# Attention over short sequences on one core: another order of TensorE's work, transposes two chunks ahead, and Q left in key order until its scores are written

## The chip, the core and the metric

The kernel runs on one core of a Trainium2 chip. A core has several engines that run side by side and wait for each other through semaphores: TensorE (PE in the profile; PEld is its loading of weights), VectorE (DVE), ScalarE (ACT), GpSimd (POOL) and SyncE (SP). Transfers between the chip's memory (HBM) and the core's working memory (SBUF) are made by 16 DMA engines; here GpSimd issues the loads and SyncE the stores. TensorE writes its results into PSUM, eight banks of 2 KB in each of 128 partitions, from which DVE and ACT read.

The metric is the device time of one execution, in microseconds (us). For the kernel before it is 156.47 us, the median of three runs (156.12 to 156.62).

## The reference

```python
batch, n_heads, seq, head_dim = 32, 12, 128, 64      # q, k, v: float32
scale = 1.0 / np.sqrt(q.shape[-1])
scores = scale * np.matmul(q, k.transpose(0, 1, 3, 2))
scores_max = np.max(scores, axis=-1, keepdims=True)
attn = np.exp(scores - scores_max)
attn = attn / (np.sum(attn, axis=-1, keepdims=True) + 1e-8)
return np.matmul(attn, v).astype(np.float32)
```

There are 32 x 12 = 384 heads, each with 128 queries, 128 keys and 64 features. Three inputs of 12.58 MB are read and one output of that size is written. The kernel leaves out the subtraction of the row's maximum and the small constant; the inputs are small enough for exp without it. The row sums come out of the second matmul, through a column of ones behind the values.

## The kernel before

**Chunks.** The heads are handled 16 at a time, in 24 chunks (NCH = 24; A = 4 groups of partitions by CB = 4 heads each). A partition of a loaded Q or K tile holds runs of 16 consecutive rows of a head (4 KB of float32 in HBM), and a partition of a V or output tile runs of 4 rows (1 KB). These long runs mean that rows of a head are spread over partitions in an order of their own, and each step has to keep track of it.

**Loads.** All loads are issued at the start of the program by GpSimd (load_qk at L67, load_v at L75) and convert float32 to bf16 on the way. The input pool has as many buffers as there are chunks, so no load waits for compute. Their order is Q and K of chunk 0, V of chunk 0, then V, Q, K of chunks 1, 2 and so on; for the last chunk Q and K come before V, which is loaded in two halves.

**The work on a chunk c**, by function:
- turn(c, 0) and turn(c, 1), L102, DVE: two transposes each (one for each half of the 64 features, J = 2), which bring the features of Q and of K onto the partitions. Each writes 128 x 512 bf16 elements. The output pattern differs: ORDER[0] for Q puts the queries in output order, "tp g th", and so writes with a step of 4 elements in the innermost direction; ORDER[1] for K leaves "tp th g", whose innermost 8 elements are contiguous.
- scores(c), L114: 32 matmuls on TensorE, for 4 heads h, 2 feature halves j, and 4 row groups b of 32 partitions. Each writes 128 contiguous float32 of one row of s_ps. Behind them stands one exp on ACT (L119) over the whole s_ps, which gives attn in bf16. s_ps has a single buffer of four PSUM banks, so the next scores wait for this exp.
- values(c), L130 and L135: 16 matmuls with a permutation bring V's rows into the order of the keys, and ACT copies them into one of three v2 tiles, beside the column of ones.
- outputs(c, half), L147: 32 matmuls for two of the four heads. The columns of attn that they take as weights must be in output order, 32 contiguous ones for each t.
- finish(c, half, ...), L157 and L158, DVE: the reciprocal of the row sums and the multiplication into o_sb; then SyncE stores o_sb (L162), 512 KB for a chunk, or 256 KB for each half in the last two chunks.

The tiles of values and outputs share a pool of two PSUM buffers of two banks each (ps_w), in turn. The transposed tiles, attn and v2 have three buffers each, o_sb four.

**Order.** The program is scheduled by hand: each engine executes its instructions strictly in the order in which the main loop at L171 emits them. An iteration c emits scores(c), values(c+1), the Q transposes of c+1, both outputs of c, the first finish, the K transposes of c+1, the second finish. So on TensorE the outputs of c stand right behind the scores and the values that precede them, and on DVE the K transposes of c+1 stand between the two finishes of c.

Of the kernel before, what the change touches and what calls it, by code (L numbers as in the profile page):

```python
# [9 lines left out]
@with_exitstack  # L10
def kernel(
    ctx: ExitStack,
    tc: tile.TileContext,
    q: bass.AP,
    k: bass.AP,
    v: bass.AP,
    out: bass.AP,
):

    nc = tc.nc
    f32 = mybir.dt.float32
    bf16 = mybir.dt.bfloat16

    B, H, S, D = q.shape
    assert S == 128 and D == 64
    scale = 1.0 / (D ** 0.5)
    TQ = 16  # L30
    GQ = S // TQ
    T = 4
    A = 4
    G = S // T
    J = D // 32
    CB = 4
    NCH = B * H // (A * CB)

    def runs(x, t):
        return x.rearrange("b h (g t) d -> (b h g) (t d)", t=t).rearrange(  # L40
            "(n p) x -> p n x", p=128)

    qr, kr, vr, orr = runs(q, TQ), runs(k, TQ), runs(v, T), runs(out, T)

    singles = ctx.enter_context(tc.tile_pool(name="singles", bufs=1))
    pin = ctx.enter_context(tc.tile_pool(name="pin", bufs=NCH))
    pt = ctx.enter_context(tc.tile_pool(name="pt", bufs=3))
    pa = ctx.enter_context(tc.tile_pool(name="pa", bufs=3))
    po = ctx.enter_context(tc.tile_pool(name="po", bufs=4))
    ps_s = ctx.enter_context(tc.tile_pool(name="ps_s", bufs=1, space=bass.MemoryType.PSUM))  # L50
    ps_w = ctx.enter_context(tc.tile_pool(name="ps_w", bufs=2, space=bass.MemoryType.PSUM))

    NV2 = 3
    v2s = []
    for i in range(NV2):
        v2 = singles.tile([128, A, CB, D + 1], bf16, name=f"v2_{i}")
        nc.vector.memset(v2[:, :, :, D:D + 1], 1.0)  # L57
        v2s.append(v2)

    ORDER = ("p h (tp g th) -> p tp th h g", "p h (tp th g) -> p tp th h g")  # L60

    chunks, qts, attns, osbs = {}, {}, {}, {}

    def load_qk(c):
        for src, which in ((qr, 0), (kr, 1)):
            x = pin.tile([128, TQ, D], bf16, tag="qk"[which] + "_bf", name="qk"[which] + "_bf")
            nc.gpsimd.dma_start(out=x, in_=src[:, c, :].rearrange("p (t d) -> p t d", t=TQ))  # L67
            chunks[c, which] = x

    def load_v(c, parts=1):  # L70
        x = pin.tile([128, CB, T, D], bf16, tag="v_bf", name="v_bf")
        w = CB // parts
        for i in range(parts):
            n0 = c * CB + i * w
            nc.gpsimd.dma_start(  # L75
                out=x[:, i * w:(i + 1) * w],
                in_=vr[:, n0:n0 + w, :].rearrange("p n (t d) -> p n t d", t=T))
        chunks[c, 2] = x

    with tc.manual_schedule():  # L80
        load_qk(0)
        ident = singles.tile([128, 128], bf16)
        make_identity(nc, ident)
        perm = singles.tile([128, A, 4, GQ], bf16)
        nc.vector.tensor_copy(  # L85
            perm.rearrange("p a th g -> p a g th"),
            ident.rearrange("p (a g th) -> p a g th", a=A, th=4))

        load_v(0)
        for c in range(1, NCH):  # L90
            if c < NCH - 1:
                load_v(c)
            load_qk(c)
        load_v(NCH - 1, 2)

        def turn(c, which):


            x = chunks.pop((c, which))
            xt = pt.tile([128, J, 4, S], bf16, tag="qk"[which] + "t", name="qk"[which] + "t")  # L100
            for j in range(J):
                nc.vector.transpose(  # L102
                    xt[:, j].rearrange(ORDER[which], tp=4, th=4),
                    x[:, :, j * 32:(j + 1) * 32].rearrange("p (th tp) e -> p tp th e", tp=4))
            qts[c, which] = xt

        def scores(c):
            qt, kt = qts.pop((c, 0)), qts.pop((c, 1))
            s_ps = ps_s.tile([128, 4, 4, S], f32, tag="s_ps", name="s_ps")
            for h in range(4):  # L110
                for j in range(J):
                    for b in range(4):
                        pr = slice(b * 32, (b + 1) * 32)
                        nc.tensor.matmul(  # L114
                            s_ps[:, b, h, :], lhsT=kt[pr, j, h, :],
                            rhs=qt[pr, j, h, :], start=(j == 0), stop=(j == J - 1),
                            tile_position=(b * 32, 0))
            attn = pa.tile([128, 4, 4, S], bf16, tag="attn", name="attn")
            nc.scalar.activation(out=attn, in_=s_ps, func=mybir.ActivationFunctionType.Exp,  # L119
                                 bias=0.0, scale=scale)  # L120
            attns[c] = attn

        def values(c, n0=0, w=CB):

            v_bf = chunks[c, 2]
            v_ps = ps_w.tile([128, 1024], f32, tag="w_ps", name="v_ps")
            vp = v_ps[:, :A * w * D].rearrange("p (a n d) -> p a n d", a=A, n=w)
            for a in range(A):
                for t in range(T):
                    nc.tensor.matmul(  # L130
                        vp[t * G:(t + 1) * G, a],
                        lhsT=perm[:, a].rearrange("p th g -> p (th g)"),
                        rhs=v_bf[:, n0:n0 + w, t, :], start=True, stop=True,
                        tile_position=(0, t * G))
            nc.scalar.copy(v2s[c % NV2][:, :, n0:n0 + w, :D], vp)  # L135

        def outputs(c, half):
            attn = attns[c]
            v2 = v2s[c % NV2]
            o_ps = ps_w.tile([128, 1024], f32, tag="w_ps", name="o_ps")  # L140
            o2 = o_ps.rearrange("p (i x) -> p i x", i=2)
            ov = o2[:, :, :T * (D + 1)].rearrange("p i (t e) -> p i t e", t=T)
            for i in range(2):
                n = 2 * half + i
                for t in range(T):
                    for a in range(A):
                        nc.tensor.matmul(  # L147
                            ov[a * G:(a + 1) * G, i, t, :], lhsT=attn[:, n, a, t * G:(t + 1) * G],
                            rhs=v2[:, a, n, :], start=True, stop=True, tile_position=(0, a * G))
            return ov  # L150

        def finish(c, half, ov, store):
            if half == 0:
                osbs[c] = po.tile([128, CB, T, D], f32, tag="o_sb", name="o_sb")
            o_sb = osbs[c]
            recip = pa.tile([128, 2, T], f32, tag="recip", name="recip")
            nc.vector.reciprocal(recip, ov[:, :, :, D])  # L157
            nc.vector.tensor_mul(o_sb[:, 2 * half:2 * half + 2], ov[:, :, :, :D],  # L158
                                 recip.to_broadcast([128, 2, T, D]))
            if store:  # L160
                n0, n1 = 2 * (half + 1) - store, 2 * (half + 1)
                nc.sync.dma_start(  # L162
                    out=orr[:, c * CB + n0:c * CB + n1, :],
                    in_=o_sb[:, n0:n1].rearrange("p n t d -> p n (t d)"))

        e = NCH - 1
        turn(0, 0)
        turn(0, 1)
        scores(0)
        values(0)  # L170
        for c in range(e):  # L171
            if c > 0:
                scores(c)
            if c + 1 < e:
                values(c + 1)
            turn(c + 1, 0)
            o0 = outputs(c, 0)
            o1 = outputs(c, 1)
            finish(c, 0, o0, 2 if c == e - 1 else 0)
            turn(c + 1, 1)  # L180
            finish(c, 1, o1, 2 if c == e - 1 else CB)
        scores(e)
        values(e, 0, 2)
        values(e, 2, 2)
        o0 = outputs(e, 0)
        finish(e, 0, o0, 2)
        o1 = outputs(e, 1)
        finish(e, 1, o1, 2)
# [30 lines left out]
```

## Time and profile before

| | |
|---|---|
| time, median of three runs | 156.47 us (156.12 to 156.62) |
| the profiled execution, time | 156.66 us |
| the profiled execution, span | 154.9 us |
| busy: DVE / PE / ACT / POOL | 126.0 / 82.7 / 68.1 / 44.9 us |
| HBM read / written | 37.75 / 12.58 MB |
| mean granted TensorE clock | 0.549 of full speed |

The span runs from the first to the last instruction of the profile; the execution's own time is 1.76 us longer. The page divides the span into 40 slices and gives the busy share of each engine in tenths. The chain of work that ended last is followed back from the last instruction: at each step to what released it. In a row of the groups stand the line, the engine and operation, the tiles written and read with their shapes, the count, then the busy time with the mean duration of one in ns, then the idle time of the engine just before them and what ended most of it. In a row of the timeline or the chain stand the start and the duration in us first. A row of the windows gives the busy time (and count) of PE, PEld, DVE, ACT and POOL, the clock, the DMA engines' share and the GB/s.

### The profile page before, as it was taken

What the parts mean: (1) busy time and instruction counts of PE and PEld (TensorE: products, weight loads), DVE (VectorE), ACT (ScalarE), POOL (GpSimd) and SP (SyncE); (2) the same over time, 40 slices, a digit from 0 to 9 for tenths busy, and PEclk for the clock granted to TensorE, in tenths of its full rate; (3) what the DMA queues carried; (4) which work ended last, traced back from release to release, by engine and by line L of the source; (5) the groups of instructions that cost most, each with busy time, mean ns of one, the idle gap of its engine ahead of it and who ended that gap; (6) DMA issues with size and microseconds to landing.
All of it is one profiled execution on the core that took longest, in us unless ns stands there. A gap on an engine that the chain in (4) does not pass through costs nothing.

```text
span 154.9 us, 5909 instructions
## 1 busy us (share of the span) xinstructions
PE 82.7 (53%) x2704; PEld 53.5 (35%) x2704; DVE 126.0 (81%) x196; ACT 68.1 (44%) x50; POOL 44.9 (29%) x79
## 2 busy tenths in 40 slices
PE   0082565565565566556656556645746746644630
PEld 0051343343343343343343344333424424423420
DVE  1719988988988988988988988987988988988731
ACT  3054527527427427437337337337247256254150
POOL 7934434243333332331432332342231100000000
PEclk9999555555555555555555555555555555555555
DMA  3999999999999999999999999999999998134123
GB/s 47 172 189 204 206 223 231 247 228 237 243 229 232 247 229 231 245 230 228 247 229 228 247 229 231 244 229 232 248 225 236 237 248 227 38 134 138 69 72 135
DMA packets 32329, 31.84 MB, mean 206 GB/s; under 512 B 1584, under 2 KB 26160, under 8 KB 32304
## 3 DMA queue, kind: packets, MB, share of 16 engines
q0 software_dynamic: 19600, 18.88, 73.6%
q1 hardware_dynamic: 12704, 12.58, 28.2%
q8 instruction: 21, 0.34, 0.8%
q14 instruction: 4, 0.03, 0.1%
HBM read 37.75 MB, written 12.58 MB: 325 GB/s over the span
## 4 chain that ended last, share of the span: by engine, by line
DVE 34%; ACT 28%; PE 24%; DMA 5%; issue 4%; POOL 2%; ACTq 1%; POOLq 0%
ACT attn L119 28%; DVE kt L102 18%; PE s_ps L114 14%; DVE o_sb L158 11%; PE o_ps L147 10%; DMA q_bf<-in_q_dram 5%; DVE recip L157 3%; DVE qt L102 2%; POOL v_bf L75 1%; POOL k_bf L67 0%; ACTq L214 0%; POOL q_bf L67 0%; ACTq L119 0%; POOL ident masks.py:199 0%; POOL ident masks.py:197 0%
## 5 line engine op out<-in xcount | busy, mean ns | idle before, releaser
L119 ACT ACTIVATE attn<-s_ps 128x2048 bf16<-128x2048 f32 x24 | 45.0, 1877 | 80.5 <-PE s_ps L114 80.5
L102 DVE STREAM_TRANSPOSE qt<-q_bf 128x512 bf16<-128x512 bf16 x48 | 58.0, 1302 | 4.9 <-DMA q_bf<-in_q_dram 4.9
L114 PE MATMUL s_ps<-qt,kt 32*128 32x128 bf16 x768 | 29.4, 302 | 34.3 <-DVE kt L102 34.3
L147 PE MATMUL o_ps<-v,attn 128*32 128x65 bf16 x1536 | 29.9, 241 | 32.9 <-ACT attn L119 24.6
L147 PEld LDWEIGHTS <-attn 128*32 128x32 bf16 x1536 | 23.3, 125 | 46.7 <-ACT attn L119 36.5
L158 DVE TENSOR_TENSOR o_sb<-o_ps,recip 128x512 f32<-128x512 f32 x48 | 33.2, 691 | 1.7
L114 PEld LDWEIGHTS <-kt 32*128 32x128 bf16 x768 | 18.6, 129 | 42.3 <-DVE kt L102 42.3
L102 DVE STREAM_TRANSPOSE kt<-k_bf 128x512 bf16<-128x512 bf16 x48 | 31.1, 685 | 0.0
L130 PE MATMUL v_ps<-v_bf,perm 128*32 128x256 bf16 (+1 forms) x400 | 25.1, 406 | 0.3 <-DMA v_bf<-in_v_dram 0.3
L75 POOL DMA_DIRECT2D v_bf<-in_v_dram x25 | 18.8, 753 | 21.1 <-DMA q_bf<-in_q_dram 17.7
L135 ACT CAST v<-v_ps 128x1024 bf16<-128x1024 f32 (+1 forms) x25 | 24.2, 978 | 0.0
L67 POOL DMA_DIRECT2D k_bf<-in_k_dram x24 | 12.8, 534 | 38.3 <-DMA v_bf<-in_v_dram 37.4
L157 DVE RECIPROCAL recip<-o_ps 128x8 f32<-128x8 f32 x48 | 9.0, 188 | 16.0 <-PE o_ps L147 16.0
L67 POOL DMA_DIRECT2D q_bf<-in_q_dram x24 | 12.9, 539 | 16.0 <-DMA k_bf<-in_k_dram 13.8
L130 PEld LDWEIGHTS <-perm 128*32 128x32 bf16 x400 | 11.6, 130 | 7.4 <-issue 4.5
L85 DVE COPY perm<-ident 128x128 bf16<-128x128 bf16 x1 | 0.4, 446 | 2.0 <-POOL ident masks.py:199 2.0
L119 ACT ACT_TABLE_LOAD x1 | 1.3, 1283 | 0.7 <-PEq L203 0.7
L57 DVE MEMSET v<- 128x16 bf16 x3 | 0.2, 72 | 0.9 <-PEq L203 0.9
masks.py:199 POOL TENSOR_SCALAR_AFFINE_SELECT ident<-ident 128x128 bf16<-128x128 bf16 x1 | 0.3, 287 | 0.1
masks.py:197 POOL MEMSET ident<- 128x128 bf16 x1 | 0.2, 231 | 0.0
L203 POOL MEMSET const-float32-0.0<- 128x1 f32 x1 | 0.1, 93 | 0.2 <-issue 0.2
L203 POOL MEMSET const-bfloat16-1.0<- 128x1 bf16 x1 | 0.1, 95 | 0.0
(2 smaller groups left out, 0.2 us busy)
## 6 DMA issues: line engine op xcount, KB each, us to landing
out_dram<-o_sb SPq DMA_DIRECT2D x22, 512.0 KB, 9.1
q_bf<-in_q_dram POOLq DMA_DIRECT2D x24, 256.0 KB, 14.5
k_bf<-in_k_dram POOLq DMA_DIRECT2D x24, 256.0 KB, 13.5
v_bf<-in_v_dram POOLq DMA_DIRECT2D x23, 256.0 KB, 14.3
out_dram<-o_sb SPq DMA_DIRECT2D x4, 256.0 KB, 2.2
v_bf<-in_v_dram POOLq DMA_DIRECT2D x2, 128.0 KB, 13.5
```

The costliest lines, as they stand in the source:

```text
L57: nc.vector.memset(v2[:, :, :, D:D + 1], 1.0)
L67: nc.gpsimd.dma_start(out=x, in_=src[:, c, :].rearrange("p (t d) -> p t d", t=TQ))
L75: nc.gpsimd.dma_start(out=x[:, i * w:(i + 1) * w], in_=vr[:, n0:n0 + w, :].rearrange("p n (t d) -> p n t d", t=T))
L85: nc.vector.tensor_copy(perm.rearrange("p a th g -> p a g th"), ident.rearrange("p (a g th) -> p a g th", a=A, th=4))
L102: nc.vector.transpose(xt[:, j].rearrange(ORDER[which], tp=4, th=4), x[:, :, j * 32:(j + 1) * 32].rearrange("p (th tp) e -> p tp th e", tp=4))
L114: nc.tensor.matmul(s_ps[:, b, h, :], lhsT=kt[pr, j, h, :], rhs=qt[pr, j, h, :], start=(j == 0), stop=(j == J - 1), tile_position=(b * 32, 0))
L119: nc.scalar.activation(out=attn, in_=s_ps, func=mybir.ActivationFunctionType.Exp, bias=0.0, scale=scale)
L130: nc.tensor.matmul(vp[t * G:(t + 1) * G, a], lhsT=perm[:, a].rearrange("p th g -> p (th g)"), rhs=v_bf[:, n0:n0 + w, t, :], start=True, st ...
L135: nc.scalar.copy(v2s[c % NV2][:, :, n0:n0 + w, :D], vp)
L147: nc.tensor.matmul(ov[a * G:(a + 1) * G, i, t, :], lhsT=attn[:, n, a, t * G:(t + 1) * G], rhs=v2[:, a, n, :], start=True, stop=True, tile_ ...
L157: nc.vector.reciprocal(recip, ov[:, :, :, D])
L158: nc.vector.tensor_mul(o_sb[:, 2 * half:2 * half + 2], ov[:, :, :, :D], recip.to_broadcast([128, 2, T, D]))
```

## The change

Three things are changed.

1. The Q transposes take K's output pattern: the queries stay in the order "tp th g", as the keys do. ORDER is gone.
2. The score matmuls put them right: the right-hand operand is read in its own order, and the output in PSUM is addressed so that query (tp, th, g) lands at (tp, g, th). In the innermost direction, 8 elements g are then written with a step of 4 float32. exp, outputs and everything behind see s_ps as before.
3. The main loop is emitted in another order. Both turns of chunks 0 and 1 come first. An iteration c emits scores(c+1), both outputs of c, values(c+2), the Q transposes of c+2, the first finish of c, the K transposes of c+2, the second finish. The values of chunk 1 come in the first iteration, and those of the last chunk, in two halves, in the last one.

```diff
-    ORDER = ("p h (tp g th) -> p tp th h g", "p h (tp th g) -> p tp th h g")
...
                 nc.vector.transpose(
-                    xt[:, j].rearrange(ORDER[which], tp=4, th=4),
+                    xt[:, j].rearrange("p h (x g) -> p x h g", g=GQ),
                     x[:, :, j * 32:(j + 1) * 32].rearrange("p (th tp) e -> p tp th e", tp=4))
...
                         nc.tensor.matmul(
-                            s_ps[:, b, h, :], lhsT=kt[pr, j, h, :],
-                            rhs=qt[pr, j, h, :], start=(j == 0), stop=(j == J - 1),
+                            s_ps[:, b, h, :].rearrange("p (tp g th) -> p tp th g", tp=4, th=4),
+                            lhsT=kt[pr, j, h, :],
+                            rhs=qt[pr, j, h, :].rearrange("p (tp th g) -> p tp th g", tp=4, th=4),
+                            start=(j == 0), stop=(j == J - 1),
                             tile_position=(b * 32, 0))
...
         e = NCH - 1
-        turn(0, 0)
-        turn(0, 1)
+        for c in range(2):
+            turn(c, 0)
+            turn(c, 1)
         scores(0)
         values(0)
         for c in range(e):
-            if c > 0:
-                scores(c)
-            if c + 1 < e:
-                values(c + 1)
-            turn(c + 1, 0)
+            scores(c + 1)
+            if c == 0:
+                values(1)
             o0 = outputs(c, 0)
             o1 = outputs(c, 1)
+            if c + 2 < e:
+                values(c + 2)
+            elif c + 1 == e:
+                values(e, 0, 2)
+                values(e, 2, 2)
+            if c + 2 <= e:
+                turn(c + 2, 0)
             finish(c, 0, o0, 2 if c == e - 1 else 0)
-            turn(c + 1, 1)
+            if c + 2 <= e:
+                turn(c + 2, 1)
             finish(c, 1, o1, 2 if c == e - 1 else CB)
-        scores(e)
-        values(e, 0, 2)
-        values(e, 2, 2)
         o0 = outputs(e, 0)
         finish(e, 0, o0, 2)
         o1 = outputs(e, 1)
```

## The prediction

> **What bounds the kernel now.** I read the page's slices first, then the chain of waits, then GpSimd's timeline, which dates the landing of each load.
>
> ```profile
> span 154.9 us, 5909 instructions
> PE 82.7 (53%) x2704; PEld 53.5 (35%) x2704; DVE 126.0 (81%) x196; ACT 68.1 (44%) x50; POOL 44.9 (29%) x79
> ...
> DMA  3999999999999999999999999999999998134123
> GB/s 47 172 189 204 206 223 231 247 228 237 243 229 232 247 229 231 245 230 228 247 229 228 247 229 231 244 229 232 248 225 236 237 248 227 38 134 138 69 72 135
> ```
>
> Two things are nearly full: DVE, and the DMA engines up to slice 33. A slice is 154.9/40 = 3.87 us, so the loads are over at about 34 x 3.87 = 132 us. The last 23 us are compute that has fallen behind, with only stores left. One period of the chain, in order of time:
>
> ```profile
> 114.25 0.69 DVE o_sb L158
> 114.94 1.22 DVE kt L102 x2
> 116.17 0.05 issue
> 116.21 0.96 PE s_ps L114 x28
> 117.26 1.89 ACT attn L119
> 119.19 0.66 PE o_ps L147 x31
> 119.87 0.22 DVE recip L157
> 120.11 0.69 DVE o_sb L158
> ```
>
> It is a closed loop: K transposes, scores, exp, first half of the outputs, reciprocal, multiply, then the next K transposes. It takes 120.11 - 114.25 = 5.86 us and runs through three engines one after another. Within it DVE also does the Q transposes, while ACT and PE work. The groups give the work per chunk:
>
> ```profile
> L119 ACT ACTIVATE attn<-s_ps 128x2048 bf16<-128x2048 f32 x24 | 45.0, 1877 | 80.5 <-PE s_ps L114 80.5
> L102 DVE STREAM_TRANSPOSE qt<-q_bf 128x512 bf16<-128x512 bf16 x48 | 58.0, 1302 | 4.9 <-DMA q_bf<-in_q_dram 4.9
> L114 PE MATMUL s_ps<-qt,kt 32*128 32x128 bf16 x768 | 29.4, 302 | 34.3 <-DVE kt L102 34.3
> ...
> L158 DVE TENSOR_TENSOR o_sb<-o_ps,recip 128x512 f32<-128x512 f32 x48 | 33.2, 691 | 1.7
> ...
> L102 DVE STREAM_TRANSPOSE kt<-k_bf 128x512 bf16<-128x512 bf16 x48 | 31.1, 685 | 0.0
> ...
> L157 DVE RECIPROCAL recip<-o_ps 128x8 f32<-128x8 f32 x48 | 9.0, 188 | 16.0 <-PE o_ps L147 16.0
> ```
>
> DVE per chunk is (58.0 + 31.1 + 33.2 + 9.0)/24 = 5.47 us, so even without the loop DVE would allow little less than 5.86. Now the loads:
>
> ```profile
> 11.94 2.45 DVE L102 STREAM_TRANSPOSE qt<-q_bf 128x512 bf16<-128x512 bf16 x2 [3.48 <-DMA q_bf<-in_q_dram]
> 12.20 0.75 POOL L75 DMA_DIRECT2D v_bf<-in_v_dram  x1 [0.74 <-DMA q_bf<-in_q_dram]
> 13.43 0.53 POOL L67 DMA_DIRECT2D q_bf<-in_q_dram  x1 [0.49 <-DMA k_bf<-in_k_dram]
> ...
> 17.29 0.53 POOL L67 DMA_DIRECT2D q_bf<-in_q_dram  x1 [0.52 <-DMA k_bf<-in_k_dram]
> ...
> 114.83 0.53 POOL L67 DMA_DIRECT2D k_bf<-in_k_dram  x1 [0.93 <-DMA k_bf<-in_k_dram]
> ```
>
> The loads are all issued by GpSimd without waiting for compute, in the order q0 k0 v0 v1 q1 k1 v2 q2 k2 and so on, and each issue waits for the load eight places ahead of it: Q of chunk 1 landed at 11.94 (DVE starts on it), and the issue eight places behind starts at 12.20. So a landing is an issue start less 0.26 us: K(1) at 13.17, K(2) at 17.03, K(20) at 114.57. Before any store is under way a chunk of loads takes **L = 17.03 - 13.17 = 3.86 us**. The stores:
>
> ```profile
> 17.19 6.18 SPq L162 DMA_DIRECT2D out_dram<-o_sb  x2
> ...
> 111.14 40.68 SPq L162 DMA_DIRECT2D out_dram<-o_sb  x10
> ...
> out_dram<-o_sb SPq DMA_DIRECT2D x22, 512.0 KB, 9.1
> ...
> k_bf<-in_k_dram POOLq DMA_DIRECT2D x24, 256.0 KB, 13.5
> ...
> 136.00:142.00 6.00, 2.49 (x96) 1.75 (x96) 5.37 (x9) 2.93 (x3) 0.00 (x0) 0.50 0.29 98
> ```
>
> Ten stores from 111.14 on are those of chunks 16 to 21 and two each of 22 and 23. At 114.57 stores 0 to 15 have landed (store 15 was issued one period earlier, at 105.28, and 9.1 us is the median to landing), and 3.43/9.1 = 0.38 of store 16. From K(2) to K(20), 97.54 us, 18 chunks of loads and 16.38 stores were moved, so a store takes **S = (97.54 - 18 x 3.86)/16.38 = 1.71 us** from the loads. With stores alone (last row: 98 GB/s at a share of 0.29, so 338 GB/s when busy) 524 KB take 1.55 us, near enough: the two kinds share one throughput. A balanced chunk costs DMA 3.86 + 1.71 = **5.57 us**, only 0.29 less than the loop's 5.86. This is what will cap the gain.
>
> **The change, part by part.** *Q in key order.* The Q transposes get the output pattern that the K transposes have (runs of 8 contiguous elements instead of a step of 4), in the same count and size, so I price them by the K row: 685 for 1302 ns, 48 times, 29.6 us less DVE work in all. DVE per chunk becomes (2 x 31.1 + 33.2 + 9.0)/24 = 4.35 us.
>
> *Score matmuls write in output order.* The step of 4 moves from DVE's output to TensorE's: in PSUM each fp32 goes 16 bytes behind its predecessor, and runs of 8. The right-hand operand is still read contiguously. No matmul of the trace writes with a step, so I bound it. Below: no cost; a gain is excluded since nothing is shortened. Above: the only row with this very pattern is the Q transpose, 1302/685 = 1.9 times. I take the 1.9, as that row is the same pattern and all others are contiguous: 0.96 us of scores in the chain become 1.82, so +0.86 us per chunk. TensorE has room for it in the steady state: the loop that will hold it is values 1.05, scores 1.82, first outputs 0.66, reciprocal and multiply 0.22 + 0.69, some 0.2 for four hand-overs (0.05 each, the issue row of the chain), 4.64 us, under 5.57. Without that cover it would cost 23 x 0.86 = 20 us. In the tail it shows once, 0.86.
>
> ```profile
> 111.21 1.05 PE L130 MATMUL v_ps<-v_bf,perm 128*32 128x256 bf16 x16
> ...
> 146.37 1.05 PE L130 MATMUL v_ps<-v_bf,perm 128*32 128x128 bf16 x32
> ...
> 148.33 1.08 ACT L135 CAST v<-v_ps 128x512 bf16<-128x512 f32 x2
> ...
> 150.73 0.69 DVE L158 TENSOR_TENSOR o_sb<-o_ps,recip 128x512 f32<-128x512 f32 x1
> ...
> L135 ACT CAST v<-v_ps 128x1024 bf16<-128x1024 f32 (+1 forms) x25 | 24.2, 978 | 0.0
> ```
>
> The Trainium skill speaks against this edit: its page "PSUM — Partial Sum Buffer", section Specifications (TRN2), gives PSUM 8-byte cachelines and says that any non-contiguous pattern slows matmuls significantly, without a factor. If each fp32 needs a line of its own where two shared one, an estimate from that page is 2 times, and the sum below would move by another 0.1 us; if the page were wrong here, it would fall by 0.86. No run here shows a matmul of that kind.
>
> *PE order and turns two ahead.* Scores of c+1 now stand ahead of the outputs of c, and their transposes were made one iteration earlier, so the exp of a chunk runs under the outputs of the one before and the 5.86 us loop is cut open. What is left is four separate limits per chunk: DVE 4.35; ACT (45.0 + 24.2)/24 = 2.88; the TensorE loop 4.64 as above (values of c+2 wait for the PSUM buffer that the first half's multiply frees); DMA 5.57. No instruction or DMA is added. The three buffers of the transposed tiles, of attn and of the values suffice for one more chunk ahead, since the tile written belongs to a chunk three back whose readers stand earlier in PE's order. SP's stores keep their order and GpSimd's queue isn't touched.
>
> What it adds is a wait: DVE's finish of c stands behind the transposes of c+2, which wait for loads. Behind the wait are the reciprocal and multiply, behind them the PSUM buffers, the values of c+2 and the store of c. In the steady state this only sets the lag: store c goes out a K transpose pair (1.22) and one finish (0.22 + 0.69) after K(c+2) lands, plus about 0.3 since the pair for Q and the first finish (2.13) don't quite fit between the landings of Q and K (a third of L to a third of L + S, 1.29 to 1.86). That is K(c+2) + 2.5 us, and the first store moves from 17.2 to about 17.03 + 2.5 = 19.5 us.
>
> **The sum.** From K(2) on, DMA is never empty. K(23) lands after 20.67 more chunks of loads (the last V comes behind it). By then stores 0 to 18 are done; 19 was issued at K(21) + 2.5. K(22) to K(23) is only Q and K (2/3 of 3.86, with stores about 4.0 us), so store 19 is 5.57 + 4.0 - 2.5 = 7.1 us old, 0.78 of it done, and store 20 is 1.5 old, 0.17 done: 19.95. K(23) = 17.03 + 20.67 x 3.86 + 19.95 x 1.71 = 17.03 + 79.8 + 34.1 = **130.9**.
>
> From there to the end, each step after the one it waits for: K pair starts +0.3, done +1.55; scores done +3.45 (1.82 and hand-over); first outputs of 22 +4.1; their finish +5.05; second finish of 22 +5.95; the second values half (0.52) +6.5, and in PE's order o0 of 23 (0.66) +7.2, o1 +7.85; finishes of 23 +8.1 and +9.05. The casts of half a chunk (0.54 each) and the exp (1.89, done +5.4) lie beside this. The last V needs its 1.29 us and the 1.05 + 0.83 shares of stores 19 and 20, so it is there at about +3, ahead of its use at +5.1. After DVE's last row the present kernel ends 154.9 - 151.42 = 3.48 us later. So +9.05 + 3.5 = 12.55, and the span is 143.4. The profiled execution took 156.66 us for 154.9, 1.76 outside, and lies 0.19 above the median 156.47: **145.2**, and for the median 145.0.
>
> **Rivals.**
> *The strided write costs far more* (slower). The TensorE loop is X + 2.82 us with X the scores. It reaches the present 5.86 at X = 3.04, 3.2 times now. At 4 times, X = 3.84, the period is 6.66: 156.5 + 23 x 0.80 + 2.9 in the tail = 178. For it speaks only that no row shows such a write; against it that DVE, doing the same, lost 1.9. Chance 0.06, not less, because that row is another engine and another memory. The rule of the Trainium skill's page "PSUM — Partial Sum Buffer" named above has no factor, and so doesn't exclude it.
> *Q's transposes stay at 1302 ns*, because it is not the output step that slows them. Then DVE needs 5.47, still under 5.57, so DMA sets the pace all the same, but the last K pair starts some 1.5 us later (1.22 more in the Q pair, and the finish behind it): 146.5. Chance 0.10; the two rows differ in nothing else that I see.
> *Loads don't feel more stores.* If the load queue runs at its present pace whatever the stores do, K(23) lands where it does now, 114.83 + 13.5 = 128.3, and the end is 142.4. Against it: a chunk of loads took 3.86 without stores and 97.54/18 = 5.42 with them. Chance 0.10.
> *No change*: 156 needs K(23) 11 us later, at 141.9, a store then costing (141.9 - 96.8)/19.95 = 2.26 us. The tail row's 1.55 speaks against it. Chance 0.04.
>
> **How the numbers follow.** My forecast, DMA at 5.57 per chunk and then a 12.5 us tail, has 0.70. Its own range is 143 to 148. The range 141.5 to 149.5 takes in no cost of the strided write (144.1), the second and third rival, S at 1.55 (-3.2, 141.8), and a strided write near 3 times with S at 1.85 (+1.1 and +2.8). A measurement of this kernel tells about 0.3% from no change. Faster: the forecast, rivals two and three, and part of the unnamed rest, 0.91; same 0.03; slower 0.06.
>
> **What would show it.** Q transposes at about 685 ns; the L114 rows longer, 28 matmuls in about 1.8 instead of 0.93 us; DVE's idle time put down to DMA of Q and K, not to PE; exp no longer in a chain of 5.86; DMA at 9 in every slice until about 131 us, and a last slice group much shorter than 23 us. If DVE waits for PE and DMA slices drop below 9 in the middle, the strided write binds and I am wrong; if the loads end at 128, the sharing of DMA was wrong.

## The result and the profile after

The changed kernel takes 146.34 us (median of four runs, 145.71 to 147.09) against 156.55 us for the kernel before on the same chip: a ratio of 0.935, with a 95% interval of 0.929 to 0.941. The forecast was 145.0, in a range of 141.5 to 149.5. Here and below a median and its range are over all runs of a kernel, and a ratio compares fast runs alone, since some runs fall into a slower state.

From the page of the changed kernel: span, busy times, DMA slices, queues, and groups.

```profile
span 143.9 us, 5908 instructions
PE 87.9 (61%) x2704; PEld 59.9 (42%) x2704; DVE 100.4 (70%) x196; ACT 70.6 (49%) x50; POOL 44.9 (31%) x79
...
DMA  2999999999999999999999999999999999998444
...
q8 instruction: 21, 0.34, 0.9%
...
L119 ACT ACTIVATE attn<-s_ps 128x2048 bf16<-128x2048 f32 x24 | 45.0, 1877 | 33.7 <-PE s_ps L112 33.7
L112 PE MATMUL s_ps<-qt,kt 32*128 32x128 bf16 x768 | 43.9, 436 | 17.0 <-DVE kt L100 13.4
L100 DVE STREAM_TRANSPOSE qt<-q_bf 128x512 bf16<-128x512 bf16 x48 | 31.2, 689 | 24.1 <-DMA q_bf<-in_q_dram 24.1
...
L147 PE MATMUL o_ps<-v,attn 128*32 128x65 bf16 x1536 | 25.8, 229 | 19.6 <-issue 18.4
```

DMA is now at 9 until slice 36, so for 36 x 3.6 = 130 us of a span of 143.9, where 23 us of stores and compute used to follow. The Q transposes take 689 ns instead of 1302. DVE has 25.6 us less to do (126.0 to 100.4) and now waits 24.1 us for Q from DMA, as the forecast wanted. The exp waits 33.7 us for the scores instead of 80.5: the loop is open. The score matmuls are slower, 436 ns in the mean instead of 302. One row wasn't in the forecast: TensorE stands still for 18.4 us before output matmuls with "issue" as the reason, that is, for nothing the profile shows.

The end, from the timeline of the changed kernel (start, duration, then in brackets the idle time before):

```profile
125.50 1.30 DVE L100 STREAM_TRANSPOSE qt<-q_bf 128x512 bf16<-128x512 bf16 x2 [1.45 <-DMA q_bf<-in_q_dram]
...
131.40 0.21 DVE L157 RECIPROCAL recip<-o_ps 128x8 f32<-128x8 f32 x1 [0.39 <-PE o_ps L147]
...
132.25 1.29 DVE L100 STREAM_TRANSPOSE kt<-k_bf 128x512 bf16<-128x512 bf16 x2
...
133.61 0.28 PE L112 MATMUL s_ps<-qt,kt 32*128 32x128 bf16 x1 [0.30 <-DVE kt L100]
...
134.16 0.94 PE L112 MATMUL s_ps<-qt,kt 32*128 32x128 bf16 x27 [0.28 <-issue]
...
139.78 0.69 DVE L158 TENSOR_TENSOR o_sb<-o_ps,recip 128x512 f32<-128x512 f32 x1
```

The last K transposes start at 132.25, not when K lands but behind a finish that waits 0.39 us for TensorE; the last multiply ends at 140.47, and the span 3.4 us later. The chain of waits shows where this end begins; these are its last wait for a load and two stops of TensorE behind it:

```profile
99.62 14.90 DMA q_bf<-in_q_dram
...
120.28 1.30 issue
...
125.47 2.40 issue
```

From 114.52 on, it runs through DVE and TensorE and the two stops, and no longer through the landing of a load.

### The profile page after: what moved, and what is told of

Read it like the earlier page. It is cut to its first block, busy times and chain, and to the rows that moved or that the text cites. A ratio compares the mean times of both kernels' runs of the same rounds, so it can differ in the third digit from the quotient of the medians.

```text
span 143.9 us, 5908 instructions
## 1 busy us (share of the span) xinstructions
PE 87.9 (61%) x2704; PEld 59.9 (42%) x2704; DVE 100.4 (70%) x196; ACT 70.6 (49%) x50; POOL 44.9 (31%) x79
## 4 chain that ended last, share of the span: by engine, by line
DMA 74%; PE 10%; issue 6%; DVE 5%; POOL 3%; POOLq 0%
DMA q_bf<-in_q_dram 36%; DMA k_bf<-in_k_dram 20%; DMA v_bf<-in_v_dram 18%; PE s_ps L112 5%; DVE o_sb L158 3%; PE o_ps L147 3%; PE v_ps L130 2%; POOL v_bf L73 2%; DVE kt L100 1%; DVE recip L157 1%; DVE qt L100 1%; POOL k_bf L65 0%; POOL q_bf L65 0%; POOL ident masks.py:199 0%; POOL ident masks.py:197 0%
## 5 line engine op out<-in xcount | busy, mean ns | idle before, releaser
L119 ACT ACTIVATE attn<-s_ps 128x2048 bf16<-128x2048 f32 x24 | 45.0, 1877 | 33.7 <-PE s_ps L112 33.7
L112 PE MATMUL s_ps<-qt,kt 32*128 32x128 bf16 x768 | 43.9, 436 | 17.0 <-DVE kt L100 13.4
L100 DVE STREAM_TRANSPOSE qt<-q_bf 128x512 bf16<-128x512 bf16 x48 | 31.2, 689 | 24.1 <-DMA q_bf<-in_q_dram 24.1
L112 PEld LDWEIGHTS <-kt 32*128 32x128 bf16 x768 | 29.0, 169 | 29.4 <-DVE kt L100 20.8
L135 ACT CAST v<-v_ps 128x1024 bf16<-128x1024 f32 (+1 forms) x25 | 24.5, 980 | 33.7 <-PE v_ps L130 33.7
L147 PE MATMUL o_ps<-v,attn 128*32 128x65 bf16 x1536 | 25.8, 229 | 19.6 <-issue 18.4
L147 PEld LDWEIGHTS <-attn 128*32 128x32 bf16 x1536 | 20.6, 118 | 29.7 <-issue 27.9
L130 PE MATMUL v_ps<-v_bf,perm 128*32 128x256 bf16 (+1 forms) x400 | 22.5, 360 | 15.1 <-DVE o_sb L158 13.2
L130 PEld LDWEIGHTS <-perm 128*32 128x32 bf16 x400 | 10.8, 118 | 20.4 <-DVE o_sb L158 15.7
L65 POOL DMA_DIRECT2D q_bf<-in_q_dram x24 | 12.9, 539 | 18.4 <-DMA k_bf<-in_k_dram 16.3
## 6 DMA issues: line engine op xcount, KB each, us to landing
k_bf<-in_k_dram POOLq DMA_DIRECT2D x24, 256.0 KB, 14.2
```

Source lines behind the costliest of these rows:

```text
L100: nc.vector.transpose(xt[:, j].rearrange("p h (x g) -> p x h g", g=GQ), x[:, :, j * 32:(j + 1) * 32].rearrange("p (th tp) e -> p tp th e", ...
L112: nc.tensor.matmul(s_ps[:, b, h, :].rearrange("p (tp g th) -> p tp th g", tp=4, th=4), lhsT=kt[pr, j, h, :], rhs=qt[pr, j, h, :].rearrange ...
L130: nc.tensor.matmul(vp[t * G:(t + 1) * G, a], lhsT=perm[:, a].rearrange("p th g -> p (th g)"), rhs=v_bf[:, n0:n0 + w, t, :], start=True, st ...
L147: nc.tensor.matmul(ov[a * G:(a + 1) * G, i, t, :], lhsT=attn[:, n, a, t * G:(t + 1) * G], rhs=v2[:, a, n, :], start=True, stop=True, tile_ ...
```

## Experiments

### The two halves of the change, each alone

The order of the main loop alone; transposes and score matmuls as before (the edit is shown against the changed kernel, cut):

```diff
-                    xt[:, j].rearrange("p h (x g) -> p x h g", g=GQ),
+                    xt[:, j].rearrange(ORDER[which], tp=4, th=4),
...
-                            s_ps[:, b, h, :].rearrange("p (tp g th) -> p tp th g", tp=4, th=4),
+                            s_ps[:, b, h, :],
```

> Only the new order of the main loop; Q transposes write with the step of 4 again and the score matmuls write contiguously, as before. Theory (DMA sets the pace, 3.86 us of loads + 1.71 of a store per chunk = 5.57, and DVE at 5.47 per chunk still fits under it): 145.5 to 148, so nearly the whole gain. Rival (the gain came from the 29.6 us taken off DVE): DVE binds again and most of the gain goes, 152 or more.

Measured: 147.45 us (147.35 to 148.53), ratio 0.944 (0.940 to 0.948). From its page:

```profile
PE 79.0 (54%) x2704; PEld 54.1 (37%) x2704; DVE 124.1 (85%) x196; ACT 70.4 (48%) x50; POOL 44.9 (31%) x79
```

The new order alone brings 9.1 of the 10.2 us, although DVE is nearly as heavily loaded as before (124.1 us busy for 126.0). The rival falls: the work taken off DVE is worth 1.1 us at most.

Q in key order and the strided score write alone, with the old main loop (the first two of the three changes, put into the kernel before):

> Only Q in key order with the score matmuls writing at a step of 4; the main loop as before. Theory (the old loop of K transposes, scores, exp, outputs, finish is closed and holds the scores; 28 score matmuls go from 0.93 to 1.68 us as in the trace of after): the period goes from 5.86 to about 6.6, 156.5 + 23 x 0.75 = 173 to 175, slower than before although DVE has 29.6 us less to do. Rival (DVE's load was the bound): about 150 or less.

Measured: 172.34 us, ratio 1.102 (1.098 to 1.106). One period of its chain of waits:

```profile
50.36 1.89 ACT attn L121
52.29 0.66 PE o_ps L149 x28
52.97 0.22 DVE recip L159
53.21 0.69 DVE o_sb L160
53.91 1.22 DVE kt L102 x2
55.13 0.05 issue
55.17 1.71 PE s_ps L114 x25
56.97 1.89 ACT attn L121
```

The loop is the old one with 1.71 us of scores in place of 0.96: 56.97 - 50.36 = 6.61 us. DVE is busy for only 99.3 of 171.1 us in this kernel. In the closed loop the edit that lightens DVE costs 16 us: the Q transposes that it shortens weren't in the loop, and the scores that it lengthens were.

### What a strided write costs, and where it shows

The kernel before with four write patterns, by chunk (one run, 165.22 us):

```diff
-                        nc.tensor.matmul(
-                            s_ps[:, b, h, :], lhsT=kt[pr, j, h, :], ...
+                        if c % 4 == 0:
+                            nc.tensor.matmul(s, **kw)
+                        elif c % 4 == 1:
+                            nc.tensor.matmul(s.rearrange("p (x two) -> p two x", two=2), **kw)
+                        elif c % 4 == 2:
+                            nc.tensor.matmul(
+                                s.rearrange("p (x u two) -> p u x two", u=2, two=2), **kw)
+                        else:
+                            nc.tensor.matmul(
+                                s.rearrange("p (tp g th) -> p tp th g", tp=4, th=4), **kw)
```

> The kernel before, with the score matmuls of a chunk writing in one of four patterns by c mod 4: contiguous; a step of 2 float32 (8 bytes); pairs of contiguous float32 with a step of 4 (16 bytes); the step of 4 of the changed kernel. The queries of a head come out in other orders (this leaves out their order). In this kernel the granted clock is 0.5 from about 15 us on, so the rows compare. Theory A (a write is as fast as contiguous where two neighbouring float32 share 8 bytes): pairs take as long as contiguous, 28 matmuls in 0.93 us, step 2 and step 4 both about 1.7. Theory B (any break of contiguity costs the same): pairs are as slow as step 4. Theory C (the cost grows with the step): step 2 lies between.

Measured, in its timeline; the lines are L118 contiguous, L120 a step of 2, L122 pairs, L125 the step of 4:

```profile
41.32 1.68 PE L120 MATMUL s_ps<-qt,kt 32*128 32x128 bf16 x28 [0.19 <-DVE kt L102]
...
47.93 0.93 PE L122 MATMUL s_ps<-qt,kt 32*128 32x128 bf16 x28 [0.30 <-DVE kt L102]
...
53.79 1.68 PE L125 MATMUL s_ps<-qt,kt 32*128 32x128 bf16 x28 [0.20 <-DVE kt L102]
...
60.40 0.93 PE L118 MATMUL s_ps<-qt,kt 32*128 32x128 bf16 x28 [0.30 <-DVE kt L102]
```

Theory A holds, and B and C fall. A step of 2 costs as much as a step of 4, 1.68 against 0.93 us or 1.8 times, and pairs of neighbours with jumps between them cost nothing. What counts in these four patterns is whether two float32 written one after the other lie side by side, in the same 8 bytes (pairs across such a boundary were not tried). The Trainium skill's page "PSUM — Partial Sum Buffer", section Specifications (TRN2), gives these 8-byte lines, and the trace agrees; that any non-contiguous pattern slows a matmul, as it also says, is too strong: the pairs are non-contiguous and take 0.93. One part of the expectation did not hold: the granted clock on record in this run is 1.00 from 20 to 40 us and 0.95 from 40 to 90. The contiguous rows take the 0.93 us of the kernel before all the same, and after 90 us, where 0.55 is on record, the four patterns still take 0.93 and 1.68, so the four compare.

The changed kernel with contiguous score writes:

```diff
-                            s_ps[:, b, h, :].rearrange("p (tp g th) -> p tp th g", tp=4, th=4),
-                            lhsT=kt[pr, j, h, :],
-                            rhs=qt[pr, j, h, :].rearrange("p (tp th g) -> p tp th g", tp=4, th=4),
+                            s_ps[:, b, h, :], lhsT=kt[pr, j, h, :], rhs=qt[pr, j, h, :],
```

> The changed kernel, but the score matmuls write contiguously: this leaves out putting the queries of a head into output order. Theory (the slower write is hidden in the steady state and shows only at the end, where the scores of the last two chunks stand in the chain): 28 score matmuls in 0.93 us or less instead of 1.68, 0.8 to 1.7 us less time, 144.6 to 145.5. Rival (TensorE's loop holds the pace in the steady state): 5 us or more less.

Measured: 146.29 us, ratio 0.935 (0.932 to 0.938): no difference from the changed kernel. The rival falls, but so does the theory's 0.8 to 1.7 us at the end. In this run's profile Q of chunk 22 lands at 126.75 instead of 125.50, and the last multiply ends at 140.50 instead of 140.47; the end is shorter by what its start is later. Why that load was later in it isn't settled.

### What the loads cost the engines, and the engines the loads

The changed kernel with half the stores:

```diff
-            if store:
+            if store and (c % 2 == 0 or c >= e - 1):
```

> The changed kernel without the stores of the odd chunks 1 to 21 (11 stores of 512 KB are left out, all compute stays). Theory (loads and stores share one throughput, a store costs the loads 1.71 us): DMA needs 4.72 us per chunk, just above TensorE's loop of 4.64: 11 x 1.71 = 18.8 us less, 127.5 to 130. Rival (loads don't feel the stores, or an engine sets the pace): 143 or more.

Measured: 141.22 us, ratio 0.903 (0.899 to 0.907), 5.1 us less than the changed kernel and not 18. Neither theory gives that. The DMA slices of this run's page, and then rows of TensorE's timeline:

```profile
DMA  2999999999999999999999999999999930404044
```

```profile
95.81 1.47 PE L112 MATMUL s_ps<-qt,kt 32*128 32x128 bf16 x24 [1.74 <-issue]
...
102.12 0.61 PE L112 MATMUL s_ps<-qt,kt 32*128 32x128 bf16 x8 [0.78 <-issue]
...
108.19 0.98 PE L147 MATMUL o_ps<-v,attn 128*32 128x65 bf16 x57 [0.73 <-issue]
...
113.99 0.52 PE L147 MATMUL o_ps<-v,attn 128*32 128x65 bf16 x41 [1.05 <-issue]
...
119.78 0.62 PE L130 MATMUL v_ps<-v_bf,perm 128*32 128x256 bf16 x16 [0.60 <-DVE o_sb L158]
```

DMA did what the sharing said: it is full for 32 slices of 3.48 us, so the loads are over at about 111 us instead of 130 in the changed kernel. But compute didn't follow. DVE's K transposes start at 98.74, 104.20, 109.62 and 115.15, 5.47 us apart, and then, with the loads over, at 119.64, 123.70 and 127.76, 4.2 apart. In the first stretch TensorE stops about once per chunk with nothing to wait for, and the place of the stop wanders: it comes after 8 scores, 24 scores, 7 outputs and 23 outputs. With 32 scores, 64 outputs and 16 values matmuls in a chunk these are 128, 127 and 128 matmuls apart, each with its weight load: some 256 instructions. In the changed kernel's page queue q8 moves instructions in 21 pieces, and 2 x 2704 matmuls and weight loads over 21 are 258 each. That gave a new theory: TensorE's next block of instructions comes through the same DMA engines, and is late while they are full of loads.

Then the same with contiguous score writes, so that TensorE should have 0.75 us less to do per chunk:

> The changed kernel without the stores of the odd chunks 1 to 21 and with score matmuls that write contiguously (so it also leaves out the queries' output order). With half the stores DMA needs 4.72 us per chunk and no longer sets the pace (141.2 us, 5.45 per chunk). Theory (TensorE's loop with the slower write and the stops then sets it, and DMA at 5.57 hid that in the changed kernel): the write's 0.75 us per chunk shows now, a period of 4.7 to 4.9, 128 to 133. Rival (something else holds 5.45, or the write is hidden there too): 139 to 142.

Measured: 140.77 us (139.3 to 147.0), ratio 0.897 (0.892 to 0.902), as with the slower write; the old theory falls. The period between K transposes from 64.71 to 108.47 is 5.47 us again. TensorE's working time doesn't seem to hold the pace, but alone this is a weak test: in this stretch its busy time is lower by only 2.1 us than in the run before (25.90 for 27.98), since this profile has fewer of the quick matmuls described at the end.

No loads beyond the first three chunks, which all later chunks use again:

```diff
-        for c in range(1, NCH):
-            if c < NCH - 1:
-                load_v(c)
-            load_qk(c)
-        load_v(NCH - 1, 2)
+        for c in range(1, 3):
+            load_v(c)
+            load_qk(c)
...
-            x = chunks.pop((c, which))
+            x = chunks[c % 3, which]
```

> The changed kernel, but only chunks 0 to 2 are loaded and every later chunk computes on one of these three (so 21 of 24 chunks of loads are left out; all compute and all stores stay). It asks what the engines need per chunk, and whether TensorE's stops that wait for nothing the profile shows (every 127 matmuls or so, 0.7 to 4 us each in the run with half the stores) come from the DMA engines being full of loads. Theory (TensorE's next block of instructions comes through the same DMA engines and is late while these are full): the stops nearly vanish, a period of 4.1 to 4.7 us, 17 + 22 x 4.4 + 10 = 120 to 125. Rival (the stops belong to TensorE's own instruction stream whatever DMA does): a period of 5.4 as in the run with half the stores, 140 or more.

Measured: 117.92 us (two runs, 117.19 and 118.66), a little under the expected range. From its page:

```profile
PE 66.5 (57%) x2704; PEld 45.2 (39%) x2704; DVE 97.5 (83%) x196; ACT 70.6 (60%) x50; POOL 6.3 (5%) x15
...
DMA  1999910505522541453255145315504532541652
```

The stops are gone: no idle time before a matmul is put down to "issue" in its waits. DVE is busy 97.5 of the 116.9 us and runs at 4.06 us per chunk (K transposes at 59.67, 63.73, 67.79). This is what the engines need, with TensorE at a granted clock of 0.95 in this run. The DMA engines are full only in the first slices.

Two runs change the number of TensorE's instructions. The first puts 32 matmuls of a single column per chunk among the outputs, the second streams the outputs' columns with half the matmuls; both on the kernel with half the stores and contiguous writes:

```diff
+                        if a % 2 == 0:
+                            nc.tensor.matmul(
+                                o2[a * G:(a + 1) * G, i, 400:401], lhsT=ident[:, :32],
+                                rhs=ident[:, :1], start=True, stop=True, tile_position=(0, a * G))
```

> The kernel with half the stores and contiguous score writes (140.8 us; it leaves out 11 stores and the queries' order), and 32 more tiny matmuls per chunk among the outputs (one column each, into an unused column of PSUM): 64 more rows in TensorE's stream of some 225 per chunk, at little engine time (some 0.02 us each, 0.6 us per chunk; the slower write's 0.75 us per chunk cost nothing there). Theory (TensorE is held by the supply of its instructions, some 6.2 us for a block of 256 while loads fill the DMA engines): the period goes from about 5.5 to 289/256 x 6.2 = 7.0 until the loads are over, 155 to 170. Rival (the stops are not a matter of the number of instructions): 140 to 146.

```diff
-                for t in range(T):
+                for t in range(0, T, 2):
...
-                            ov[a * G:(a + 1) * G, i, t, :], lhsT=attn[:, n, a, t * G:(t + 1) * G],
-                            rhs=v2[:, a, n, :], start=True, stop=True, tile_position=(0, a * G))
+                            ov[a * G:(a + 1) * G, i, t:t + 2, :], lhsT=attn[:, n, a, t * G:(t + 1) * G],
+                            rhs=v2[:, a, i:i + 2, :], start=True, stop=True, tile_position=(0, a * G))
```

> The same base (half the stores, contiguous score writes), with the 64 output matmuls of 65 columns per chunk made into 32 of 130 columns, which write the same places in PSUM from other heads' values (so it also leaves out correct outputs): the columns streamed stay, the weight loads and matmuls halve, 161 rows per chunk instead of 225. Theory (instruction supply): 161/256 x 6.2 = 3.9 us per chunk, under DMA's 4.72, so DMA sets the pace as first predicted for half the stores: 127.5 to 131. Rival (the streaming time of TensorE, or another engine, holds 5.45): 138 to 141.

Measured: 156.66 us (155.34 to 159.25) with the filler and 128.92 us (128.79 to 129.08), ratio 0.824 (0.821 to 0.826), with fewer instructions. Both are where the theory had them, the first at its lower end: the period is 6.66 us (K transposes from 63.84 to 97.12 in five periods), not 7.0, so a block took 5.9 us there and not 6.2, and this lasts only until the loads are over. The working time of the filler doesn't account for the 15.9 us more: TensorE's busy time rises by only 6.4 us, from 78.0 to 84.4 (at mean granted clocks of 0.600 and 0.759). From the pages, the instruction queue with fewer instructions and with the filler; then from the waits (engine, line, reason, then us in total, times, longest) with fewer instructions, of the base, and with the filler:

```profile
q8 instruction: 15, 0.25, 0.7%
...
q8 instruction: 27, 0.44, 1.1%
```

```profile
PE o_ps L145 <- issue: 0.3, 1, 0.3
```

```profile
PE o_ps L145 <- issue: 18.3, 9, 3.0
...
PE s_ps L112 <- issue: 6.5, 4, 1.7
...
PE v_ps L128 <- issue: 2.8, 2, 1.6
```

```profile
PE o_ps L145 <- issue: 21.6, 11, 3.6
...
PE o_ps L149 <- issue: 8.4, 5, 2.9
...
PE v_ps L128 <- issue: 6.8, 3, 2.9
...
PE s_ps L112 <- issue: 6.3, 5, 3.0
```

From 21 blocks to 15 the stops vanish, 27.6 us in all in the base; and then half the stores give the 128.9 us that DMA's sharing had first predicted for it (4.68 us per chunk from 50.58 to 116.12, for a forecast of 4.72). From 21 to 27 they grow to 43.1 us, 15.5 more, and the time by 15.9. So both halves of the theory stand: loads and stores share one throughput, and while it is full TensorE is held to a block of some 256 instructions in about 6 us (5.47 x 256/225 = 6.2 without the filler, 5.9 with it). Two kernels with full DMA engines use their blocks more slowly and don't show the stops: in the kernel before a block lasts 5.86 x 256/225 = 6.7 us, with fewer instructions 4.68 x 256/161 = 7.4, and in the waits of the first no matmul stands behind "issue", in those of the second one, for 0.3 us. The Trainium skill's page "Runtime: NRT & Kernel Launch", section Instruction fetch mechanics, has the blocks of 256 instructions fetched through a DMA queue, which fits. It calls the cost mostly hidden, which it is here in the kernel before and in the run with fewer instructions, and not where a full DMA meets a faster use of instructions: 27.6 us in the base.

Which of the two limits holds the changed kernel itself? The merged outputs again, with all stores and the slower write:

> The changed kernel with all stores, and only the output matmuls merged as in the run with 32 of 130 columns (it leaves out correct outputs): 161 rows of instructions per chunk instead of 225. It asks which of the two nearly equal limits holds the changed kernel. Theory (DMA's 5.57 us per chunk does; the instruction supply at 5.45 lies just under it): at most 2 us less, 144.3 to 146.3. Rival (the instruction supply holds it): 4 us or more less, 142 or below.

Measured: 145.82 us (143.78 to 146.09), ratio 0.928 (0.923 to 0.932).

```profile
L100 DVE STREAM_TRANSPOSE qt<-q_bf 128x512 bf16<-128x512 bf16 x48 | 31.3, 690 | 32.5 <-DMA q_bf<-in_q_dram 32.5
```

No matmul waits for "issue" any more, and DVE waits 32.5 us for Q instead of 24.1. The stops cost the changed kernel 0.5 us by the medians and 1.1 by the two ratios, and the rival's 4 us lie outside the interval: DMA holds it, as forecast, with the instruction supply 0.1 us per chunk behind.

### The end

The last K transposes ahead of both finishes of chunk 21:

```diff
+            if c + 2 == e:
+                turn(e, 1)
             finish(c, 0, o0, 2 if c == e - 1 else 0)
-            if c + 2 <= e:
+            if c + 2 < e:
                 turn(c + 2, 1)
```

> The changed kernel with one move: in iteration 21 the last K transposes stand ahead of both finishes of chunk 21 on DVE. Theory (after the last K has landed DVE's order sets the end: in the trace of after the K transposes start at 132.25, behind a finish that waits for PE, and could start at 131.0): 1.0 to 1.4 us less, 145.0 to 145.4. Rival (the end hangs on the last landing or on TensorE): no difference, 146.0 to 146.6.

Measured: 146.81 us, ratio 0.939 (0.937 to 0.941): no gain. From its timeline:

```profile
121.84 1.30 DVE L100 STREAM_TRANSPOSE qt<-q_bf 128x512 bf16<-128x512 bf16 x2 [3.42 <-DMA q_bf<-in_q_dram]
...
127.61 1.30 DVE L100 STREAM_TRANSPOSE qt<-q_bf 128x512 bf16<-128x512 bf16 x2 [1.62 <-DMA q_bf<-in_q_dram]
...
134.72 1.05 PE L112 MATMUL s_ps<-qt,kt 32*128 32x128 bf16 x32 [1.23 <-ACT attn L119]
```

From the landing of Q of chunk 22 to the last multiply it takes 140.56 - 127.61 = 12.95 us instead of 14.97, so that stretch is shorter. The move itself took the distance between the last Q and the last K transposes from 2.53 to 1.21 us, and part of it went into a new wait of 1.23: the last scores now wait for the exp before, since there is one buffer of scores. But in this profile the Q of chunk 22 landed 2.1 us later. What decides when the last loads land within these 2 us stays open.

Three stores held back until that of chunk 20, with eight output buffers:

```diff
+                if c in (17, 18, 19):
+                    late.append((c, n0, n1))
+                    return
+                put(c, n0, n1)
+                if c == 20:
+                    for x in late:
+                        put(*x)
```

> The changed kernel with the stores of chunks 17, 18 and 19 issued behind that of chunk 20 (eight output buffers instead of four), so that the loads end earlier and these stores run under the last chunks. Theory (loads and stores share one throughput; TensorE's instruction supply is quick again once the loads are over): the loads end 4 to 5 us earlier, the last chunks run at 4.1 us, 1 to 2 us less, 144.3 to 145.3. Rival (the pace until then is the instruction supply's, or the stores are late at the end): 146 or more.

Measured: 145.94 us, ratio 0.932 (0.930 to 0.934), above the theory's range: 0.4 us under the changed kernel's median, whose runs span 1.4, so not a gain I would claim. The last multiply ends at 139.52, 0.95 earlier, but the span is at 144.4, 4.9 us after it instead of 3.4. That the held-back stores were in the way of the last ones fits (the 256 KB stores take 4.1 us to land in the median instead of 2.4), but no run separates it. No version clearly beats the changed kernel with the whole computation.

## Why the prediction was right, point by point

**What bounds it.** Right. The closed loop of 5.86 us was what held the kernel before, and opening it gave nearly the whole gain (147.45 with the loop's order alone). DMA took its place.

**DMA's price per chunk.** Right. The issues of GpSimd date the landings again:

```profile
12.83 0.53 POOL L65 DMA_DIRECT2D q_bf<-in_q_dram  x1 [0.49 <-DMA k_bf<-in_k_dram]
...
16.68 0.53 POOL L65 DMA_DIRECT2D q_bf<-in_q_dram  x1 [0.54 <-DMA k_bf<-in_k_dram]
...
116.32 0.53 POOL L65 DMA_DIRECT2D k_bf<-in_k_dram  x1 [0.99 <-DMA k_bf<-in_k_dram]
```

With the same 0.26 taken off, L is 16.68 - 12.83 = 3.85. K(20) lands at 116.06, 99.64 us after K(2). Some 17.3 stores were done by then (the one of chunk 17 was issued at 112.63, a store takes 9.5), so S = (99.64 - 18 x 3.85)/17.3 = 1.75. The forecast had 3.86 and 1.71.

**Q in key order.** Right: 689 ns against the 685 of the K row. That its worth is small, because DVE fitted under DMA with 5.47 as well, was the point of the second rival, and the order alone bore it out: 147.45 where that rival said 146.5. The sizes were too large: 29.6 us and 5.47 and 4.35 per chunk add up durations and groups that overlap. DVE's busy time fell by 25.6 us, and it needs 126.0/24 = 5.25 us per chunk before and 97.5/24 = 4.06 in the run with three chunks of loads.

**The strided write.** The size was right (28 matmuls from 0.93 to 1.68 us, 1.8 times where 1.9 was taken). The 0.86 us that it was to add at the end did not show: contiguous writes take the same time. In the changed kernel's last chunk 28 of these matmuls ran from 133.61 to 135.10, 1.5 us, so the faster of two speeds helped there (below).

**TensorE's loop.** This is the term that was mis-sized: 4.64 us per chunk by its own rows, 5.47 measured with half the stores, because the sum had no row for the supply of instructions. The profile before could not show it, since a block lasted 6.7 us there. The forecast's margin under DMA, 0.93 us, was really 0.1. That it did no harm is luck: DMA still lay just above.

**The sum.** The total is right, but the path of its last part is not the one forecast. K's last transposes were to start at 130.9 + 0.3 = 131.2 and started at 132.25, behind the finish that waited for TensorE; from there to the last multiply it took 8.22 us instead of 8.75. The forecast had the landing of the last K release them. That landing stands in no row; an estimate from its issue at 116.32 and the median of 14.2 us to landing is 130.5, near the 130.9, but 1.7 us ahead of the start. What released them was TensorE's work on the chunks before. It is so without stops too: with the merged outputs the last load in the chain is the Q of chunk 22, landing at 125.38 us, and the last K transposes start at 131.96. That the lateness and the shorter end nearly cancel is luck. Span 143.9 for 143.4, and 145.71 us in that run for 145.2. The median lies 0.6 above its profiled run, where I had taken the 0.19 off: 146.34 for 145.0, 1.3 us or 0.9% low.

**The rivals.** A strided write at 4 times is refuted by the rows. That loads don't feel stores is refuted twice: L and S again, and 128.9 us with half the stores once the stops are gone.

## What to carry to other kernels

Look first for a closed loop through several engines: opening it was worth 9 us, and making a step outside it cheaper at the price of a step inside it cost 16. When the bound moves, list each new limit with its distance, and count instructions as one of them: here loads and stores (5.57 us per chunk), the supply of TensorE's instructions (5.47) and DVE (4.06) lay in that order, so of the next saving in DMA, some 18 us, the second let only 5 through. A strided PSUM write cost nothing here where pairs of float32 stayed together (0.93 us in both).

## What was not expected of the hardware

**TensorE's instructions compete with loads.** While the DMA engines are full, a block of some 256 instructions comes about every 6 us; the stops, of up to 3.9 us in the run with half the stores, are marked "issue", come 127 or 128 matmuls apart in its rows above, and vanish with the loads.

**Two speeds of the same matmuls.** In the changed kernel 28 strided score matmuls take 1.68 us in some chunks and 0.94 in others, contiguous ones 0.94 and 0.57 in the run with contiguous writes. In the changed kernel the granted clock on record goes with it: 1.00 from 22 to 26 us, around a row of 0.94, and 0.50 from 111.2 to 113.6, around one of 1.68. But the record doesn't always fit. In the run with four patterns, from its windows (span in us, then busy times and counts, then the clock, the DMA share and the GB/s),

```profile
40.00:90.00 50.00, 30.81 (x896) 19.62 (x896) 42.11 (x66) 22.26 (x16) 16.54 (x28) 0.95 1.20 233
```

it is 0.95 where the contiguous rows take 0.93 us; and the kernel before, with 0.549 in its profile, has 1.0 in nearly all of its executions beside these experiments, at the same 156 us. What gives a run more of the faster speed isn't shown. It isn't TensorE's busy share alone: with the filler it is busy 54% of the span at a mean clock of 0.759, with contiguous writes 54% at 0.597, and in the changed kernel 61% at 0.720.
